# Attention on one Trainium2 core: one K chunk transposed by DMA, the loads in another order, and a new opening list

## The chip, the core and the metric

The kernel runs on one core of a Trainium2 chip. The metric is device microseconds of one execution. A core has five engines that run their own instruction streams and wait for each other by semaphores: TensorE (PE, matmuls and the loading of their weights), VectorE (DVE), ScalarE (ACT), GpSimd (POOL) and SyncE (SP), and DMA queues that SP, ACT and POOL fill. Matmuls write to PSUM, which has eight banks of 128 x 512 float32; ACT and DVE read and free them.

## What is computed

```python
"q", "k", "v": np.random.randn(8, 2048, 512).astype(np.float32)

d_k = q.shape[-1]
scores = np.matmul(q, k.transpose(0, 2, 1)) / np.sqrt(d_k)
attn_weights = special.softmax(scores, axis=-1).astype(np.float32)
return np.matmul(attn_weights, v)
```

Eight batches of attention, 2048 queries and keys of width 512, no mask.

## The kernel before

Everything is float16 on the way into PE and float32 in PSUM. Each batch's queries are cut into two spans of 1024, each span into two halves of 512. The scores are made transposed, with 128 keys on the partitions and 512 queries along a row, so that their exponentials can go straight into the second matmul as weights. K of a batch is four chunks (`kraw`, c = 0 to 3) of four blocks of 128 keys; Q is four such chunks, of which two make a span (`qraw`, one tile for each span). Both come as rows and have to be transposed, d onto the partitions.

**Seven products for eight.** A group (class `Group`, line 311) takes two key blocks and both halves of a span's queries. As a 2 x 2 block product over two halves of d it would be eight products of two matmuls; the kernel uses the form with seven, whose operands are sums. Sums of K are `k_sums(c)` (line 191: `ks`, and one in place in `kraw`), those of Q `q_sums(sp)` (line 208: `qs`, and one in place or in a spare room). Product 1 goes to a bank x; a copy puts it into a second bank y as well (`after1`); 6, 7 and 4 are added on x and 2 on y; 5 and 3 make z. After 5, z is copied to a float32 tile `cz` in SBUF (`after5`, line 362), after 6 x is copied beside it (`after6`, line 365), two adds on DVE (`after7`, `after3`, lines 368 and 371) finish the right half, and exponentials on ACT (line 279) write `left` (queries of the first half, from x and y) and `right` (second half, one wide exponential from `cz`, `exp_right`). A span has eight groups. In the first span of the first batch the sums aren't there yet when PE starts, so its first eight key blocks (chunks 0 and 1) are made without them, by `plain_eighth` and by `plain_tile` (line 281, four matmuls of 512 columns); groups 0 to 3 of the opening's steps are the other four pairs of blocks of span 0 (chunk 2 in groups 0 and 1, chunk 3 in groups 2 and 3), groups 4 to 11 are span 1.

**The second matmul** (P times V) works on two columns a and b of 128 queries of either half, also in seven products: words a1 to a7 and b1 to b7 (line 455), with sums of V (`v_sums`, line 223) and of P (`p_sums`, line 384). From the second pair of columns on, three of the seven are split once more (`fine`, line 649, words s, t, u).

**Banks.** `bank(name)` (line 83) hands out a bank from a pool: "qx" (2), "qy" (1), "qz" (1), "px" (2) and "pz" (2, also as "py"). A group's x came from "qx"; `own` said whether y and z came from the q or the p pools: p for groups 1 and 3, q for all others. `COPIES` held two letters for each group of span 0: which engine, ACT or DVE, copies y and z; x was always copied by ACT, and in span 1 all three were.

**Start.** Rows of chunk 0 come in single blocks. Then POOL's queue (lines 871 to 876) loads K chunk 1, Q chunk 1, Q chunk 2, K chunk 2, Q chunk 3, K chunk 3, the last five as 512 KB each into rooms that `left` and `right` of span 1 will use later (`spare`), so that in the profile these chunks have the names `right` and `left`. Q and K chunks 0 and 1 and K chunks 2 and 3 are transposed by PE (`transposed`, line 165: four 128 x 128 transposes for each block, and a copy from PSUM by DVE or ACT, line 173). Q chunks 2 and 3, needed by span 1, are transposed by SP's DMA queue, two halves each (`dma_transpose`, line 156, issued at line 160). POOL then copies one element of Q chunk 2's first half (`gate`, line 914); the four loads of V (line 221) stand behind that copy in POOL's queue.

**The opening list.** Up to the second pair of columns the order is written out by hand in `OPENING` (line 746), word by word (`word`, line 944), and each engine runs its own part of it in order. `*` is one step of `score()`: the next of the seven products in the order of `QORDER`, where products 7 and 4 of a group come between those of the next; the first steps of that kind with no group before are empty. `TK2.0.2ax` transposes K chunk 2 from block 0, two blocks, copied by a (ACT) or d (DVE), bank from x, z, p or q ("qx", "pz", "px", "qz"). `t6.1p` is the plain tile of key block 6, second half. `k21` and `q02` are sums (chunk 2, number 1; span 0, number 2), v, X, Y, Z sums of V, A, B, N sums of P; `a1<` and `a1>` are the two halves of product a1 over the keys; a 1 in front means the second pair of columns. From the third pair of columns (about 84 us) tables set the order; they repeat for the rest of the run and are the same in both kernels.

Of the kernel before, what the change touches and what calls it, by code (L numbers as in the profile page):

```python
# [12 lines left out]
def kernel(  # L13
# [21 lines left out]
    nc = tc.nc  # L35
# [16 lines left out]
    NJ = NKB // 2  # L52
# [5 lines left out]
    NG = NJ // 2  # L58
# [24 lines left out]
    def bank(name):  # L83
        name = "pz" if name == "py" else name
        t = psum[name].tile([P, 512], F32, tag=name)
        return t
# [37 lines left out]
    def load(what, b, c, pieces=(CH,), room=None):  # L124
        t = staged.get((what, b, c))
        if room is not None:
            t = staged[what, b, c] = room
        if t is None:
            t = staged[what, b, c] = stage.tile([P, CH, D], F16, tag="stage", name="stage")
        n = CH - sum(pieces)  # L130
        for w in pieces:
            at = c * CH + n
            nc.gpsimd.dma_start(out=t[:, n:n + w, :], in_=srcs[what][b, :, at:at + w, :])  # L133
            n += w
# [21 lines left out]
    def dma_transpose(what, b, c, h):  # L156
        src = staged.pop((what, b, c)) if h else staged[what, b, c]
        dst = raw_of(what, b, c)
        ns = slice(h * CH // 2, (h + 1) * CH // 2)
        nc.sync.dma_start_transpose(  # L160
            out=dst[:, ns].rearrange("p n c r -> p (n c) r"),
            in_=src[:, ns].rearrange("p n d -> p (n d)"),
        )
# [147 lines left out]
    class Group:  # L311


        def __init__(self, sp, j):
            self.sp, self.j = sp, j
            self.own = "q" if sp or j % 2 == 0 or j < NG else "p"

        def product(self, n):
            c, j = divmod(self.j, 2)
            a11, a12, a21, a22 = k_blocks(c)  # L320
            b11, b12, b21, b22 = q_blocks(self.sp)
            _, s1, s2, s4 = kops[c]
            t1, t2, t4 = qsum
            t3 = t3_of(self.sp)
            if n == 1:
                if self.sp not in pts:
                    new_p(self.sp)
                self.left, self.right = pts[self.sp][0:2]
                self.x = bank("qx")
            elif n == 5:  # L330
                self.z = bank(self.own + "z")
            lhs, rhs, dst = {
                1: (a11, b11, "x"),
                2: (a12, b21, "y"),
                3: (s4, b22, "z"),
                4: (a22, t4, "x"),
                5: (s1, t1, "z"),
                6: (s2, t2, "x"),
                7: (a21, t3, "x"),
            }[n]  # L340
            dst = getattr(self, dst)
            for dc in range(2):
                nc.tensor.matmul(  # L343
                    dst[:], lhs[:, j, dc, :], rhs[:, :, dc, :],
                    start=(n in (1, 5) and dc == 0), stop=(dc == 1),
                    skip_group_check=True,
                )
            getattr(self, f"after{n}", lambda: None)()
# [5 lines left out]

        def copy(self, n):

            by = "a" if self.sp else COPIES[2 * (self.j - 2) + n]
            return nc.scalar.copy if by == "a" else nc.vector.tensor_copy

        def after5(self):  # L360
            self.cz = czpool.tile([P, 2, QH], F32, tag="cz", name="cz")
            self.copy(1)(out=self.cz[:, 1, :], in_=self.z[:])  # L362

        def after6(self):
            nc.scalar.copy(out=self.cz[:, 0, :], in_=self.x[:])  # L365

        def after7(self):
            nc.vector.tensor_add(self.cz[:, 1, :], self.x[:], self.cz[:, 1, :])  # L368
# [160 lines left out]
    class Fine(Pair):  # L529
# [4 lines left out]
        early = False  # L534
# [192 lines left out]
    def placed(text):  # L727
# [14 lines left out]
        "a7'@1 b7'@2 a4'@5 u1@5 b4'@9 u2@10 s1@12 u3@12 s2@13 u4@14 s3@15 a3@15 s4@17 b3@18 "  # L742
        "a6@19 t1@23 b6@24 t2@24 t3@25 t4@27",
    )
    COPIES = "aadaaaadadad"
    OPENING = (
# [9 lines left out]
    )  # L756

    ENDS = {
# [100 lines left out]
    for n in range(1, CH):  # L859
# [5 lines left out]
    spare = [  # L865
        t[:].rearrange(form + " -> p (" + form[2:] + ")")[:, i * CH * D:(i + 1) * CH * D]
        .rearrange("p (n d) -> p n d", n=CH)
        for t, form, n in ((pts[1][1], "p j s q", 4), (pts[1][0][0], "p j q", 2))
        for i in range(n)
    ]  # L870
    load("k", 0, 1, (2, 2))
    load("q", 0, 1, room=spare[0])
    load("q", 0, 2, room=spare[2])
    load("k", 0, 2, room=spare[1])
    load("q", 0, 3, room=spare[5])
    load("k", 0, 3, room=spare[3])
    gate = const.tile([P, 1], F32)
    firsts["v"] = lambda: [load_v(0, c) for c in range(NCH)]
    nc.gpsimd.memset(vt1[:, :, H:H + 1], 1.0)
# [28 lines left out]
    plain_eighth(1, 1, 0)  # L908
    transposed("k", 1, 1, 1, dve)
    plain_eighth(1, 1, 1)  # L910
    for c in (2, 3):
        for h in range(2):
            dma_transpose("q", 0, c, h)
    nc.gpsimd.tensor_copy(out=gate[:], in_=qraw[1][:, 1, ND - 1, 0:1])  # L914
    firsts.pop("v")()

# [2 lines left out]

    prev = cur = None  # L920
    steps = [0]
    early = {}

    def score():

# [18 lines left out]
    def word(w):  # L944

        copies = {"d": dve, "a": act}
        rooms = {"x": "qx", "q": "qz", "p": "px", "z": "pz"}
        n = [int(x) for x in w if x.isdigit()]
        for _ in range(len(later)):
            later.popleft()()  # L950
        if w == "*":
            score()
        elif w[0] == "1":
            (pv if w[1] in "abstu" else sum_of)(1, w[1:])
        elif w[0] in "gR":
            if n[0] not in early:
                early[n[0]] = Group(0, n[0])
            if w[0] == "R":
                early[n[0]].exp_right()
            else:  # L960
                early[n[0]].product(n[1])
        elif w[0] == "t":
            plain_tile(n[0], n[1], rooms[w[-1]])
        elif w[0] == "T":
            transposed(w[1].lower(), n[0], n[1], n[2], copies[w[-2]], rooms[w[-1]])
        elif w[0] == "k":
            k_sums(n[0])[n[1]]()
        elif w[0] == "q":
            q_sums(n[0])[n[1]]()
        elif w[0] == "v":  # L970
            v_sums(0, n[0])[n[1]]()
        elif w[0] in "AB":
            part = {"<": (0, NG), ">": (NG, NJ)}.get(w[-1], (0, NJ))
            p_sums(0, w[0].lower(), *part)[n[0]]()
        elif w[0] in "XYZ":
            vi_sums(0, "XYZ".index(w[0]))[n[0]]()
        elif w[0] == "N":
            p_sums(1, "ab")[n[0]]()
        else:
            pv(0, w)  # L980
# [66 lines left out]
```

## Time and profile before

| | |
|---|---|
| median of 3 runs | 785.38 us (784.53 to 785.4) |
| the profiled execution, whole | 784.17 us |
| its span, first to last instruction | 782.4 us |
| DVE busy, 0 to 50 us of the span | 34.39 us |
| DVE busy, 50 to 100 us | 47.89 us |
| ACT busy, 50 to 100 us | 41.26 us |
| POOL's copies wait for Q chunk 2 | 16.7 us |
| moved by DMA | 117.65 MB, 150 GB/s mean |

The span is what the profile's rows are counted in; the execution is 1.8 us longer. Rows of a timeline give start and length in microseconds, then engine, line, operation, what it writes and reads, and how many were merged; a bracket at the end gives the idle time just before and who ended it. PE's own times are modelled from its starts, and matmuls overlap, so the distance from start to start is the safer measure.

### The profile page before, as it was taken

To read this page: it belongs to the slowest core of one execution; us is meant where nothing else is said; L and a number is where in the kernel's file an instruction comes from. 1 tells how busy PE (TensorE), PEld (TensorE's weight loads), DVE (VectorE), ACT (ScalarE), POOL (GpSimd) and SP (SyncE) were. 2 spreads that over 40 slices of the span, in tenths; PEclk is the share of its full clock that TensorE was granted. 3 is DMA by queue.
4 is the path that set the end of the run, shared out by engine and by line. 5 is a ranking of instruction groups with operands and counts; after the bars stand their busy time and mean duration, and the time that the engine had idled before them with its cause. 6 is when DMAs were issued, how large, how long until landed. Compare 5 with 4: busy or idle time off the path is not lost.

```text
span 782.4 us, 18227 instructions
## 1 busy us (share of the span) xinstructions
PE 776.1 (99%) x6598; PEld 534.6 (68%) x6598; DVE 718.9 (92%) x1605; ACT 643.6 (82%) x1339; POOL 116.1 (15%) x157
## 2 busy tenths in 40 slices
PE   8999999999999999999999999999999999999998
PEld 5467666676666666666766666676676666666677
DVE  3899999989999899998999989999899998999886
ACT  4888888888888888888888888888888888888873
POOL 4111112012021120211102121021210212100000
PEclk9999999999999999999999999999999999999999
DMA  9999993999939997499956999379993999932113
GB/s 187 188 156 164 160 202 73 191 181 189 177 56 199 177 193 147 84 186 191 193 118 113 180 185 193 100 140 191 163 191 92 152 176 187 202 62 61 49 49 115
DMA packets 212410, 117.65 MB, mean 150 GB/s; under 512 B 128480, under 2 KB 212064, under 8 KB 212320
## 3 DMA queue, kind: packets, MB, share of 16 engines
q0 software_dynamic: 52528, 51.91, 46.0%
q1 hardware_dynamic: 159504, 64.26, 42.0%
q8 instruction: 51, 0.84, 0.5%
q14 instruction: 39, 0.32, 0.1%
q10 hardware_dynamic: 288, 0.33, 0.1%
HBM read 100.73 MB, written 33.55 MB: 172 GB/s over the span
## 4 chain that ended last, share of the span: by engine, by line
PE 94%; DMA 4%; POOL 1%; issue 0%; ACT 0%; POOLq 0%
PE t L343 46%; PE t L455 30%; PE t L676 18%; DMA vh<-in_v_dram 2%; DMA right<-in_q_dram 1%; DMA qraw<-right 1%; POOL first L861 0%; POOL vh L221 0%; POOL stage L133 0%; POOL right L133 0%; ACT o L464 0%; POOL gate L914 0%; POOLq L1031 0%
## 5 line engine op out<-in xcount | busy, mean ns | idle before, releaser
L343 PE MATMUL t<-qraw,kraw 128*128 128x512 f16 x736 | 200.1, 379 | 0.2 <-ACT left L279 0.2
L464 ACT ACTIVATE o<-t,r 128x256 f32<-128x256 f32 x300 | 136.8, 480 | 71.3 <-DVE r L490 25.5
L279 ACT ACTIVATE left<-t 128x512 f16<-128x512 f32 (+1 forms) x260 | 154.2, 600 | 15.7 <-PE t L343 7.7
L343 PE MATMUL t<-qs,ks 128*128 128x512 f16 x496 | 140.7, 379 | 0.0
L279 ACT ACTIVATE right<-cz 128x1024 f16<-128x1024 f32 x124 | 131.9, 1064 | 3.5 <-DVE cz L368 3.4
L343 PEld LDWEIGHTS <-kraw 128*128 128x128 f16 x992 | 88.9, 97 | 58.9 <-issue 0.8
L455 PEld LDWEIGHTS <-right 128*128 128x128 f16 x1024 | 99.7, 98 | 33.4
L455 PEld LDWEIGHTS <-s 128*128 128x128 f16 x1056 | 100.4, 97 | 29.0
L676 PEld LDWEIGHTS <-si 128*128 128x128 f16 x1044 | 76.3, 97 | 36.4 <-issue 0.2
L343 PEld LDWEIGHTS <-ks 128*128 128x128 f16 x744 | 69.1, 97 | 42.2 <-issue 0.9
L362 ACT COPY cz<-t 128x512 f32<-128x512 f32 x121 | 70.9, 586 | 31.8 <-PE t L343 30.3
L371 DVE TENSOR_TENSOR cz<-t,cz 128x512 f32<-128x512 f32 x124 | 85.0, 686 | 9.5 <-ACT o L464 4.1
L368 DVE TENSOR_TENSOR cz<-t,cz 128x512 f32<-128x512 f32 x124 | 84.8, 684 | 5.8 <-PE t L343 5.2
L676 PEld LDWEIGHTS <-left 128*128 128x128 f16 x976 | 69.5, 97 | 21.2
L467 DVE SCALAR_TENSOR_TENSOR o<-t,r,o 128x256 f32<-128x256 f32 x148 | 69.3, 479 | 12.5 <-ACT ci L696 7.5
L353 ACT COPY t<-t 128x512 f32<-128x512 f32 x124 | 72.5, 584 | 3.8 <-PE t L343 0.6
L343 PE MATMUL t<-qraw,ks 128*128 128x512 f16 x248 | 73.6, 378 | 0.2 <-DVE cz L362 0.2
L343 PE MATMUL t<-qs,kraw 128*128 128x512 f16 x248 | 73.7, 379 | 0.0
L365 ACT COPY cz<-t 128x512 f32<-128x512 f32 x124 | 72.2, 583 | 0.3
L676 PE MATMUL t<-vh,left 128*128 128x128 f16 x732 | 70.8, 219 | 0.0
L455 PE MATMUL t<-vt,s 128*128 128x256 f16 (+1 forms) x544 | 70.5, 273 | 0.0
L455 PE MATMUL t<-vh,s 128*128 128x257 f16 x512 | 66.7, 273 | 0.0
(116 smaller groups left out, 1202.8 us busy)
## 6 DMA issues: line engine op xcount, KB each, us to landing
out_dram<-o SPq DMA_DIRECT2D x256, 128.0 KB, 3.8
vh<-in_v_dram POOLq DMA_DIRECT2D x32, 512.0 KB, 9.5
stage<-in_q_dram POOLq DMA_DIRECT2D x28, 512.0 KB, 7.2
stage<-in_k_dram POOLq DMA_DIRECT2D x28, 512.0 KB, 8.3
o<-o POOLq DMA_DIRECT2D x14, 128.0 KB, 2.7
right<-in_q_dram POOLq DMA_DIRECT2D x2, 512.0 KB, 9.8
right<-in_k_dram POOLq DMA_DIRECT2D x2, 512.0 KB, 14.8
qraw<-stage SPq DMA_TRANSPOSE x56, 6.4
```

The costliest lines, as they stand in the source:

```text
L279: nc.scalar.activation(out=out_, in_=in_, func=EXP, scale=inv_sqrt_d)
L343: nc.tensor.matmul(dst[:], lhs[:, j, dc, :], rhs[:, :, dc, :], start=(n in (1, 5) and dc == 0), stop=(dc == 1), skip_group_check=True,)
L353: self.copy(0)(out=self.y[:], in_=self.x[:])
L362: self.copy(1)(out=self.cz[:, 1, :], in_=self.z[:])
L365: nc.scalar.copy(out=self.cz[:, 0, :], in_=self.x[:])
L368: nc.vector.tensor_add(self.cz[:, 1, :], self.x[:], self.cz[:, 1, :])
L371: nc.vector.tensor_add(self.cz[:, 0, :], self.z[:], self.cz[:, 0, :])
L455: nc.tensor.matmul(dst[:, 0:width], lhs(j), rhs(j), start=(first and j == 0), stop=(j == NJ - 1), skip_group_check=True,)
L464: nc.scalar.activation(out=out_, in_=src, func=COPY, scale=r[:])
L467: nc.vector.scalar_tensor_tensor(out=out_, in0=src, scalar=r[:], in1=out_, op0=MULT, op1=ADD)
L676: nc.tensor.matmul(dst, lhs[:, j, :], rhs[:, j, :], start=(n == 1 and j == 0), stop=(j == NI - 1), skip_group_check=True,)
```

## The change

1. POOL loads K chunks 2 and 3 ahead of Q chunks 2 and 3.
2. K chunk 3 is transposed by SP's DMA queue, ahead of the two Q chunks. Its two words with 16 PE transposes and two DVE copies leave the list.
3. `OWNS` and `XOWNS` give each of the twelve groups of the first batch its pools for y and z and for x; `COPIES` has three letters for each, so x may be copied by DVE too. Groups 0 and 2 take x from "px"; groups 1 and 4 take y and z from "pz". DVE copies z of group 2 and x of group 10, all others are ACT's.
4. `OPENING` is laid anew. Behind Q chunk 1, two plain tiles (t6.0, t7.0) stand ahead of K chunk 2's first half, where five did (t7.0, t6.1, t1.1, t4.1, t0.1); the sums of K chunk 0, of V and of P, the plain tiles and the products of the second matmul stand in other places.
5. Code for two kinds of words that no list uses (g and R) is dropped.

```diff
--- before.py
+++ after.py
@@ -313,7 +313,10 @@
 
         def __init__(self, sp, j):
             self.sp, self.j = sp, j
-            self.own = "q" if sp or j % 2 == 0 or j < NG else "p"
+            n = sp * NJ + j - NG
+            self.by = COPIES[3 * n:3 * n + 3] if sp < 2 else "aaa"
+            self.own = OWNS[n] if sp < 2 else "q"
+            self.xown = XOWNS[n] if sp < 2 else "q"
 
         def product(self, n):
             c, j = divmod(self.j, 2)
@@ -326,7 +329,7 @@
                 if self.sp not in pts:
                     new_p(self.sp)
                 self.left, self.right = pts[self.sp][0:2]
-                self.x = bank("qx")
+                self.x = bank(self.xown + "x")
             elif n == 5:
                 self.z = bank(self.own + "z")
             lhs, rhs, dst = {
@@ -354,15 +357,14 @@
 
         def copy(self, n):
 
-            by = "a" if self.sp else COPIES[2 * (self.j - 2) + n]
-            return nc.scalar.copy if by == "a" else nc.vector.tensor_copy
+            return nc.scalar.copy if self.by[n] == "a" else nc.vector.tensor_copy
 
         def after5(self):
             self.cz = czpool.tile([P, 2, QH], F32, tag="cz", name="cz")
             self.copy(1)(out=self.cz[:, 1, :], in_=self.z[:])
 
         def after6(self):
-            nc.scalar.copy(out=self.cz[:, 0, :], in_=self.x[:])
+            self.copy(2)(out=self.cz[:, 0, :], in_=self.x[:])
 
         def after7(self):
             nc.vector.tensor_add(self.cz[:, 1, :], self.x[:], self.cz[:, 1, :])
@@ -742,17 +744,19 @@
         "a7'@1 b7'@2 a4'@5 u1@5 b4'@9 u2@10 s1@12 u3@12 s2@13 u4@14 s3@15 a3@15 s4@17 b3@18 "
         "a6@19 t1@23 b6@24 t2@24 t3@25 t4@27",
     )
-    COPIES = "aadaaaadadad"
+    COPIES = "aaaaaaadaaaaaaaaaaaaaaaaaaaaaaaadaaa"
+    OWNS = "qpqqpqqqqqqq"
+    XOWNS = "pqpqqqqqqqqq"
     OPENING = (
-        "TK1.2.1dz t5.0x TK1.3.1az t4.0x TQ1.0.2dp TQ1.2.1az TQ1.3.1dz t7.0x k10 q00 q01 t6.1p "
-        "t1.1z t4.1z t0.1p TK2.0.2ax TK2.2.2dp t3.1x k12 k20 * k22 k23 q03 t5.1z * * * t6.0x k21 "
-        "* t2.1p k00 k02 q02 * * TK3.0.2dz * * TK3.2.2dp * k30 * k32 k01 * * * * k33 * * k03 k13 "
-        "* k31 * t7.1p * * * * * v00 * a1< * q10 * * q11 * A0< * * v01 q12 b1< * * q13 * a1> * * "
-        "v02 v10 * * b1> * A0> X0 A1 k11 v11 * a5 A3 * * * X1 * a3 B0 A2 B1 v12 * * a2 B3 * * B2 "
-        "* a6 * b5 * v03 v13 X3 * 1Z1 1Z3 * * X2 b3 * * b2 N0 * 1z1 1a7' * b6 * 1Z2 1S2 1z2 1u1 * "
-        "1z3 1b7' * * * 1a4' * 1z4 1x1 1Z4 * * * 1S3 1b4' * 1u2 1S4 1x2 1k01 1s1 * 1u3 * 1x3 * "
-        "1s2 1y1 1u4 1x4 1k02 * 1a3 1y2 * 1Y1 1s3 1b3 1k03 1k04 1Y2 1y3 * 1t1 * 1N1 * 1s4 * 1Y3 "
-        "1a6 1Y4 1t2 1y4 * * * 1b6 * * 1N3 1t3 * * 1q1 1t4 1q2"
+        "TK1.2.1dz t5.0z TK1.3.1az t4.0p TQ1.2.1dp TQ1.0.2dx TQ1.3.1dz t6.0x t7.0p k10 TK2.0.2az "
+        "k12 t1.1z k00 q00 TK2.2.2dx t0.1p k20 q01 * * k22 t6.1z k21 * q02 k23 * * t5.1z q03 * * "
+        "* * * t3.1q * * * * * k30 * k32 k02 t4.1x * t2.1z k33 * * k31 * * k01 * * * * q10 q12 "
+        "t7.1p q11 * * * * A0< k13 * k03 v00 * * * b1< a1< v02 q13 * * A0> * * * v01 A1 v10 * * * "
+        "* a1> a5 A3 B0 * * k11 B1 * a3 v12 v11 * * X0 * B3 a2 a6 * * * b5 N0 * 1Z1 * b1> 1z1 * "
+        "A2 B2 b3 v13 * * * X1 * X3 b6 v03 * 1Z3 1S2 * * 1b7' b2 * 1S3 * 1Z2 * 1u1 1b4' 1z2 1a7' "
+        "* 1u2 * 1x1 1Z4 1z4 * * 1z3 1S4 1x3 1a4' 1u3 * * X2 * 1x2 1s1 1u4 * 1k01 1a3 1s2 1Y1 1x4 "
+        "* 1k02 * 1Y2 * 1y1 * * 1s3 1y2 1b3 1t1 1Y3 1y3 1s4 1y4 * 1k03 * 1k04 1t2 * 1q1 1N1 1t3 "
+        "1a6 * 1Y4 1b6 1q2 * 1t4 * 1N3 *"
     )
 
     ENDS = {
@@ -870,10 +874,10 @@
     ]
     load("k", 0, 1, (2, 2))
     load("q", 0, 1, room=spare[0])
+    load("k", 0, 2, room=spare[1])
+    load("k", 0, 3, room=spare[3])
     load("q", 0, 2, room=spare[2])
-    load("k", 0, 2, room=spare[1])
     load("q", 0, 3, room=spare[5])
-    load("k", 0, 3, room=spare[3])
     gate = const.tile([P, 1], F32)
     firsts["v"] = lambda: [load_v(0, c) for c in range(NCH)]
     nc.gpsimd.memset(vt1[:, :, H:H + 1], 1.0)
@@ -908,9 +912,9 @@
     plain_eighth(1, 1, 0)
     transposed("k", 1, 1, 1, dve)
     plain_eighth(1, 1, 1)
-    for c in (2, 3):
+    for what, c in (("k", 3), ("q", 2), ("q", 3)):
         for h in range(2):
-            dma_transpose("q", 0, c, h)
+            dma_transpose(what, 0, c, h)
     nc.gpsimd.tensor_copy(out=gate[:], in_=qraw[1][:, 1, ND - 1, 0:1])
     firsts.pop("v")()
...
```

Three places of the program, as its rows stand. First POOL's queue, from the loads of whole chunks to the copies that hold back V; `right` and `left` are the rooms, `qraw_116` is Q of span 1, `vh_120` V. Before:

```order
L133 DMA right<-in_q_dram 128x4x512 x2
L133 DMA right<-in_k_dram 128x4x512
L133 DMA left<-in_q_dram 128x4x512
L133 DMA right<-in_k_dram 128x4x512
L879 MEMSET vt_122 128x8
L880 MEMSET ui_128 128x4
L881 MEMSET vh_120 128x8
L914 CAST gate<-qraw_116 128x1
L221 DMA vh_120<-in_v_dram 128x4x512 x4
```

Now:

```order
L133 DMA right<-in_q_dram 128x4x512
L133 DMA right<-in_k_dram 128x4x512 x2
L133 DMA right<-in_q_dram 128x4x512
L133 DMA left<-in_q_dram 128x4x512
L883 MEMSET vt_122 128x8
L884 MEMSET ui_128 128x4
L885 MEMSET vh_120 128x8
L918 CAST gate<-qraw_116 128x1
L221 DMA vh_120<-in_v_dram 128x4x512 x4
```

K chunks 2 and 3 are second and third of these five loads, where they were third and fifth; V still waits for Q chunk 2.

Second, SP's queue from its start; `kraw_111` is K chunk 3, the next batch's chunks come from `stage`. Before:

```order
L140 DMA cz<-in_q_dram 128x512
L160 DMA_TRANSPOSE qraw_116<-right 128x8x128 x2
L160 DMA_TRANSPOSE qraw_116<-left 128x8x128 x2
L160 DMA_TRANSPOSE qraw_115<-stage 128x8x128 x2
L160 DMA_TRANSPOSE kraw_99<-stage 128x8x128
```

Now:

```order
L140 DMA cz<-in_q_dram 128x512
L160 DMA_TRANSPOSE kraw_111<-right 128x8x128 x2
L160 DMA_TRANSPOSE qraw_116<-right 128x8x128 x2
L160 DMA_TRANSPOSE qraw_116<-left 128x8x128 x2
L160 DMA_TRANSPOSE qraw_115<-stage 128x8x128 x2
L160 DMA_TRANSPOSE kraw_99<-stage 128x8x128
```

Two halves of K chunk 3 stand ahead of the four halves of Q.

Third, DVE around the first sums of chunk 3 (`ks_3_112`). Before, from the third sum of Q of span 0 (line 214) on:

```order
L214 TENSOR_TENSOR left<-qraw_115 128x1024
L371 TENSOR_TENSOR cz<-t,cz 128x512
L173 COPY kraw_111<-tr 128x1024
L368 TENSOR_TENSOR cz<-t,cz 128x512
L173 COPY kraw_111<-tr 128x1024
L362 COPY cz<-t 128x512
L195 TENSOR_TENSOR ks_3_112<-kraw_111 128x512
L197 TENSOR_TENSOR ks_3_113<-ks_3_112,kraw_111 128x512
```

Now:

```order
L214 TENSOR_TENSOR left<-qraw_115 128x1024
L198 TENSOR_TENSOR ks_2_110<-kraw_107,ks_2_109 128x512
L215 TENSOR_TENSOR qs_119<-qraw_115,qs_118 128x1024
L373 TENSOR_TENSOR cz<-t,cz 128x512
L370 TENSOR_TENSOR cz<-t,cz 128x512
L373 TENSOR_TENSOR cz<-t,cz 128x512
L195 TENSOR_TENSOR ks_3_112<-kraw_111 128x512
L370 TENSOR_TENSOR cz<-t,cz 128x512
L197 TENSOR_TENSOR ks_3_113<-ks_3_112,kraw_111 128x512
```

The two copies of chunk 3 and the copy of z after them (of group 1) are gone from here; the first sum of chunk 3 has the add of group 1's z (line 373) in front of it.

More of the change, by code (lines that the diff above doesn't have):

```diff
@@ L921 @@
     steps = [0]
-    early = {}
     def score():
@@ L954, in word @@
             (pv if w[1] in "abstu" else sum_of)(1, w[1:])
[L955 to L961, printed above, removed]
         elif w[0] == "t":
```

## The prediction, made before the changed kernel ran

> **What bounds the kernel now.** I read the page first: the busy times and the shares of the chain.
>
> ```profile
> PE 776.1 (99%) x6598; PEld 534.6 (68%) x6598; DVE 718.9 (92%) x1605; ACT 643.6 (82%) x1339; POOL 116.1 (15%) x157
> PE 94%; DMA 4%; POOL 1%; issue 0%; ACT 0%; POOLq 0%
> ```
>
> TensorE is busy for 776.1 of 782.4 us, and the chain that ended last is TensorE for 94%. So the time changes only by matrix work that goes away, or by waits of PE. Next, the table by stretch, since the change lies in the opening (to about 84 us).
>
> ```profile
> core 0: us, PE busy (x) PEld busy (x) DVE busy (x) ACT busy (x) POOL busy (x), PEclk, DMA share, GB/s
> 10.00:20.00 10.00, 9.77 (x75) 5.46 (x73) 3.92 (x8) 6.57 (x15) 0.01 (x1) 1.00 1.24 206
> 20.00:30.00 10.00, 9.74 (x69) 5.29 (x70) 7.84 (x16) 7.79 (x13) 3.16 (x5) 1.00 1.25 185
> 30.00:40.00 10.00, 9.82 (x47) 4.48 (x47) 8.99 (x19) 8.49 (x15) 0.24 (x1) 1.00 1.18 192
> 40.00:50.00 10.00, 9.83 (x61) 5.75 (x60) 9.91 (x21) 8.19 (x15) 2.51 (x6) 1.00 0.70 115
> 50.00:60.00 10.00, 10.00 (x72) 6.70 (x70) 9.64 (x21) 8.42 (x15) 0.75 (x1) 1.00 1.23 196
> ```
>
> PE has small holes from 10 to 50 us and none in the next ten; the clock is 1.00 throughout; VectorE (DVE) is nearly full from 40 us on. The holes, in PE's timeline (start, length, instruction; in brackets the idle time the profile sees):
>
> ```profile
> 13.36 1.03 PE L286 MATMUL t<-qraw,kraw 128*128 128x512 f16 x4
> 14.53 1.07 PE L170 MATMUL tr<-ident,right 128*128 128x128 f16 x16
> 15.43 4.48 PE L286 MATMUL t<-qraw,kraw 128*128 128x512 f16 x20
> 20.03 1.07 PE L170 MATMUL tr<-ident,right 128*128 128x128 f16 x16
> 23.95 1.89 PE L286 MATMUL t<-qraw,kraw 128*128 128x512 f16 x8
> 25.68 0.59 PE L343 MATMUL t<-qraw,ks 128*128 128x512 f16 x2
> 26.54 0.61 PE L170 MATMUL tr<-ident,right 128*128 128x128 f16 x8
> 26.99 0.59 PE L343 MATMUL t<-qraw,kraw 128*128 128x512 f16 x2
> 29.16 0.59 PE L343 MATMUL t<-qs,kraw 128*128 128x512 f16 x2
> 29.99 0.59 PE L343 MATMUL t<-qraw,ks 128*128 128x512 f16 x2 [0.24 <-DVE cz L362]
> 37.92 0.59 PE L343 MATMUL t<-qraw,kraw 128*128 128x512 f16 x2
> 38.69 0.59 PE L343 MATMUL t<-qraw,kraw 128*128 128x512 f16 x2 [0.18 <-ACT left L279]
> 41.71 0.38 PE L455 MATMUL t<-vh,left 128*128 128x256 f16 x2
> 42.26 0.38 PE L455 MATMUL t<-vh,left 128*128 128x256 f16 x2 [0.17 <-DMA vh<-in_v_dram]
> 45.51 1.06 PE L455 MATMUL t<-vt,s 128*128 128x257 f16 x8
> ```
>
> Matmuls overlap, so I count from start to start: eight 512-column matmuls from 23.95 to 25.68, 0.216 us each. A product of two is 0.43 us, a plain tile of four 0.86, eight transposes 0.45 (26.54 to 26.99). By that count PE loses 0.31 us before 14.53 (Q chunk 1), 20.03-15.43-20x0.216 = 0.27 before 20.03 (K chunk 2), 29.99-29.16-0.43 = 0.40 (a copy on DVE), 38.69-37.92-0.43 = 0.34 (an exponential that frees a bank), and 0.33 before 42.26 (the last V load; two 256-column matmuls are 0.22).
>
> **What is removed.** Chunk 3 of K needs 16 transposes less on PE: 2 x 0.45 = 0.90 us, straight off the bound. The two copies they fed leave DVE. Of the five waits, the first stays (Q chunk 1 still lands first). The other four lose their cause: K chunk 2 is awaited elsewhere (below); the DVE copy at 29.99 stood behind the two copies of chunk 3; the group that waited at 38.69 now takes a bank that was free earlier; V is awaited elsewhere. That is 0.27+0.40+0.34+0.33 = 1.34 us to be had.
>
> **What is added on PE.** I count the new list from 14.53. Sixteen transposes of Q and two plain tiles end at 14.53+0.90+1.73 = 17.16; then the list wants K chunk 2, now second in the load queue. The chain of waits gives when the second load landed, and what hung on it.
>
> ```profile
> 6.74 11.10 DMA right<-in_q_dram
> 17.86 8.79 DMA qraw<-right
> 26.94 2.21 POOL vh L221 x3
> 29.14 13.08 DMA vh<-in_v_dram
> ```
>
> The second load (Q chunk 2 then) landed at 6.74+11.10 = 17.84, the third (K chunk 2) by 20.0 by the PE row. All are 512 KB, so K chunk 2 now lands at 17.84 and PE waits 17.16 to 17.88: **+0.72**. Bound below: first to third took 14.5 to 20.0, 2.75 each, which would give 17.25 and a wait of 0.1. I take the row of the slot itself.
>
> Two halves of chunk 2 and two plain tiles (2.62) bring PE to 20.50; twelve products and three plain tiles (7.77) bring it to 28.27, where group 2 first reads chunk 3; 30.0 is where it needs the first sum of chunk 3, and 38.2 where group 4's product 6 needs the copy of its x. That copy stands on ScalarE (ACT) behind group 2's wide exponential, a copy and three exponentials: the sequence that before has from 32.65 on, first and last row here.
>
> ```profile
> 32.65 1.06 ACT L279 ACTIVATE right<-cz 128x1024 f16<-128x1024 f32 x1 [0.51 <-DVE cz L368]
> 35.52 0.62 ACT L353 COPY t<-t 128x512 f32<-128x512 f32 x1
> L371 DVE TENSOR_TENSOR cz<-t,cz 128x512 f32<-128x512 f32 x124 | 85.0, 686 | 9.5 <-ACT o L464 4.1
> L173 DVE COPY kraw<-tr x5: 425/681/692, 11.8 to 28.7; 128x1024 f16<-128x1024 f16 x3, 128x512 f16<-128x512 f16 x2
> ```
>
> It took 35.52+0.62-32.65 = 3.49 us. The wide exponential needs the add behind product 7 of group 2, which PE issues from 33.5 to 33.9; with the add's 0.69 and some 0.2 at the handover (estimated from the overlap of the matmuls) it can begin near 34.9 and the sequence ends at 38.4: **+0.3**, between 0 and 0.6 for a handover that is nothing or double.
>
> **The transfers.** Chunk 3's two halves go through SP's transposing queue ahead of the four halves of Q. Its load is third now and lands at 20.0, so SP starts 2.1 us later than it did at 17.86. The landings below are those of `right` (to 30 us), `left` (to 35) and `vh` (to 44), from issue.
>
> ```profile
> 17.86 5.43 SPq L160 DMA_TRANSPOSE qraw<-right  x2
> 23.32 4.38 SPq L160 DMA_TRANSPOSE qraw<-left  x2
> L160 SPq DMA_TRANSPOSE qraw<-right x2: 1353/2684/4015, 17.9 to 19.3; - x2
> DMA to landing us min/median/max: 8.3/9.9/17.1
> DMA to landing us min/median/max: 5.1/5.3/14.5
> DMA to landing us min/median/max: 7.1/10.1/13.1
> GB/s 0 39 347 277 142 195 161 186 185 201 204 208 203 206 213 201 204 209 206 203 196 199 163 138 286 239 86 67 200 191 201 191 211 195 204 206 204 45 0 0
> ```
>
> Halves landed at 17.86+8.79 = 26.65, 19.3+8.3 = 27.6, 23.32+5.1 = 28.4 and (issued about 26.4) 31.7. The last load was under way until 8.9+17.1 = 26.0, and the rate (slices of 1.1 us from 0 to 44 us) jumps to 286 GB/s at 26.4. So the first half did not need 8.8 us, it waited for the loads; then a half takes about 0.9. The new first two therefore land at about 26.7 and 27.6, before 28.27 and before DVE takes up the sums at about 29: **0**. Were the 8.8 and 8.3 their own length, they would land at 28.8 and 29.7: +0.5 at 28.27, and about +0.4 more at 30.0.
>
> The queue behind them matters more. The load of V stands on POOL behind a copy that reads the first half of Q chunk 2, which is the third half now: 28.4 at best (the old third), 30.5 if all shifts by 2.1, against 26.65. From that copy to V's last landing it took 42.22-26.65 = 15.57 us, so V is complete at 44.0 to 46.1; up to 0.9 more if a further half falls into its way, since three halves follow now, and one did. Without that wait PE would reach the second half of a1 (word a1>) at 38.5+5.6 = 44.15. It waits from nothing to 2.8; with the copy at 29.0, and a little for sharing, V is there at 44.9: **+0.7**. On DVE the second half's V sums (v10) wait in the same place, and the group adds stand behind them. V's first half is the second of four loads; with the first at 26.9+7.1 = 34.0 and the last at 42.2, 2.7 apart, it landed at 36.7, so some 39.1 now; it is needed at 39.4. Q's last half, 31.7 before and some 33 to 35 now, is needed at 34.7 by the Q sums on DVE. I count both at zero, with up to 0.8 against.
>
> **From 45 us to the end of the list** the sums, copies and products stand in another order. DVE has some 1.6 us less in all, by durations: the two K copies go (0.69 each, the DVE row above), of three copies of z or x one goes (taken at the add's 0.69), and one copy of a single Q block comes (0.42). I found no place where a sum comes after its product by the count, but DVE covers this with little room (9.64 of 10); at the tightest, the sum for u2, the margin is some 0.3. Zero, up to 0.5 against. From the third pair of columns on the program is the old one.
>
> **Sum.** -0.90-1.34+0.72+0.3+0.7 = -0.5 us. The profiled execution took 784.17, so its like would take 783.7; it lies 1.2 below the median of 785.38, and the forecast is against the median: **784.9**. A difference of 0.2% (1.6 us) is about what can be told from none here.
>
> **Rivals.**
>
> *The loads keep time* (22%). K chunk 2 lands at its mean pace (wait 0.1), V's gate opens at 28.4 (wait 0.1): -0.5-0.62-0.6 = -1.7, 783.7; with the 0.3 gone too, 783.4. For it: the pace of 2.75 us and the 286 GB/s. Against it: the slot's own 17.84, and six halves where there were four.
>
> *Slower: V late behind the transposes* (25%). The gate opens at 30.5, and one more half shares V's first microseconds: V complete at 47.0, PE waits 2.8 instead of 0.7, and K3's 0.5 comes with the same shift: -0.5+2.1+0.5 = +2.1, 787.5. It decides for slower once V is complete after about 46.3. For it: the start 2.1 us later, and SP's second issue that took 4.0 us with loads under way. Against it: the loads end at 26.0 in either order.
>
> *Nothing gained* (51% together with the forecast, within 0.2%). The new waits eat the 0.90 whole, for instance K3's halves at 28.8 and 29.7: -0.5+0.9 = +0.4, 785.8.
>
> *A transposing transfer is no match for PE* (2%, in the slower). If the halves could not overlap, each 8.8 us after the one before, chunk 3 would be whole at 20.0+17.6 = 37.6, and its sum, needed at 30.0, would hold PE about 8 us: 793. The landings at 26.65, 27.6 and 28.4 speak against it. Beside it stands the Trainium skill, VectorE: DVE Perf Modes, section The three transpose paths: 390 ns for a 128x128 block on TensorE against 1309 ns by DMA, and TensorE as the choice where PSUM will do. By that page, as an estimate, 16 blocks by DMA one after the other would be 20.9 us and the change a loss; the halves 0.9 us apart, 8 blocks each, do not agree with it.
>
> **How the numbers follow.** Faster 0.22, same 0.51, slower 0.27. The range goes from 783.3 (loads on time, all of it) to 787.2 (most of V late); the likeliest case alone spans 783.9 to 785.9.
>
> **What would show it.** 32 transposes from `right` in the profile after, not 48, and none of the DVE copies that followed them. A PE wait of 0.7 us for `right<-in_k_dram` near 17.2, or 0.1. The first half of kraw landing before 28.3, the copy that gates V near 29, a wait for vh near 44. Wrong if PE waits for kraw, if the gate opens after 30, or if after 50 us PE waits for a sum of DVE; and wrong in the other direction if neither chunk 2 nor V holds PE.

## The result, and the profile after

The changed kernel takes **792.0 us** (median of 6 runs, 791.2 to 792.9) against 785.2 us of the kernel before, measured beside it (784.5 to 785.8). The ratio is 1.0084, with a 95% interval of 1.0068 to 1.0100: slower by some 6.8 us, where 784.9 us and at most 787.2 was forecast. The profiled execution took 792.14 us, its span is 790.4 us, 8.0 more than the 782.4 of the profile before.

Where does it go? First the table by stretch, in the same columns as before.

```profile
core 0: us, PE busy (x) PEld busy (x) DVE busy (x) ACT busy (x) POOL busy (x), PEclk, DMA share, GB/s
0.00:34.00 34.00, 31.76 (x209) 18.56 (x210) 18.10 (x39) 20.85 (x39) 12.11 (x25) 1.00 1.09 183
34.00:52.00 18.00, 12.97 (x46) 5.13 (x44) 8.68 (x16) 8.55 (x15) 3.40 (x7) 0.72 1.05 149
52.00:780.00 728.00, 728.00 (x6263) 506.49 (x6262) 687.08 (x1539) 611.21 (x1281) 100.55 (x125) 1.00 0.86 149
```

From 52 us on PE is busy without a hole. All of the loss lies before, and most of it from 34 to 52 us, where PE issues 46 matmuls in 18 us and the mean granted clock is 0.72. PE's timeline there, and the finer stretches of the clock:

```profile
15.06 1.89 PE L286 MATMUL t<-qraw,kraw 128*128 128x512 f16 x8
17.85 0.62 PE L170 MATMUL tr<-ident,right 128*128 128x128 f16 x8 [0.89 <-DMA right<-in_k_dram]
...
37.47 0.59 PE L346 MATMUL t<-left,kraw 128*128 128x512 f16 x2
41.94 1.01 PE L346 MATMUL t<-qs,ks 128*128 128x512 f16 x2 [3.88 <-DVE qs L212]
43.27 1.03 PE L346 MATMUL t<-qs,ks 128*128 128x512 f16 x2 [0.32 <-DVE qs L213]
45.14 1.01 PE L346 MATMUL t<-qs,kraw 128*128 128x512 f16 x2 [0.83 <-DVE cz L370]
45.95 1.91 PE L457 MATMUL t<-vh,left 128*128 128x256 f16 x8
47.65 1.06 PE L346 MATMUL t<-qraw,ks 128*128 128x512 f16 x2
48.51 2.58 PE L346 MATMUL t<-qraw,kraw 128*128 128x512 f16 x6
50.92 1.03 PE L346 MATMUL t<-qs,ks 128*128 128x512 f16 x4
51.87 0.38 PE L346 MATMUL t<-qs,kraw 128*128 128x512 f16 x1
```

```profile
38.00:40.00 2.00, 0.06 (x1) 0.00 (x0) 0.00 (x0) 0.47 (x1) 0.00 (x0) 1.00 1.72 151
40.00:42.00 2.00, 0.06 (x1) 0.06 (x1) 0.77 (x2) 0.00 (x0) 0.69 (x1) 0.63 1.01 167
48.00:50.00 2.00, 2.00 (x6) 0.73 (x5) 1.02 (x2) 0.40 (x1) 0.62 (x2) 0.50 0.80 125
50.00:51.00 1.00, 1.00 (x4) 0.37 (x3) 0.00 (x0) 0.69 (x2) 0.00 (x0) 0.61 1.23 206
51.00:52.00 1.00, 1.00 (x6) 0.41 (x5) 0.88 (x2) 0.47 (x2) 0.00 (x0) 1.00 1.25 205
```

Counted from start to start as in the prediction: from 37.47 to 51.87 are 20 matmuls of 512 columns and 8 of 256, 20 x 0.216 + 8 x 0.109 = 5.19 us of work in 14.40 us. **9.21 us are lost.** PE waits 4.04 us for the Q sum of L212, and then, with a product of two at 0.85 us (half the pace), 0.48 and 1.02 us: 5.54 us of waits. The other 3.67 us are the clock. It was granted at 1.00 until about 40.5 us, some 2.5 us after PE had run dry, at 0.50 until about 50.8 (0.61 as the mean of 50 to 51 leaves the full clock only the last 0.2 us), and at 1.00 from there. With the 1.06 us that PE waits for K chunk 2 (15.06 + 8 x 0.216 to 17.85), less the 0.90 and 1.34 that the change removes, the sum is 8.03 us, the 8.0 of the spans. So close a fit is partly luck: smaller items are left out, such as Q chunk 1's transposes, which PE reached 0.37 us earlier (14.16 against 14.53), and they happen to cancel.

Why was the sum late? The chain of waits of the kernel after goes back from L212, which reads from both halves of Q chunk 3, to the transfers (`issue` rows left out). The row of L212 itself stands below it:

```profile
7.45 12.57 DMA right<-in_k_dram
...
20.03 1.34 SPq L160
...
21.43 3.68 SPq L160
...
25.16 1.31 SPq L160
...
26.51 1.35 SPq L160
...
27.91 1.32 SPq L160
...
29.27 11.84 DMA qraw<-left
...
41.20 0.70 DVE qs L212
```

```profile
41.20 0.69 DVE L212 TENSOR_TENSOR qs<-qraw 128x1024 f16<-128x1024 f16 x1 [6.45 <-DMA qraw<-left]
```

K chunk 3's load landed at 20.02, SP issued six halves one after the other, and the last of them, issued at 29.27, took 11.84 us to land. DVE had stood before this sum since 34.75 (41.20 less 6.45). In the profile before, the last half was issued at 26.4 and landed 5.3 us later:

```profile
L160 SPq DMA_TRANSPOSE qraw<-left x2: 1312/2171/3030, 23.3 to 26.4; - x2
DMA to landing us min/median/max: 5.1/5.2/5.3
```

What differs is its place against V. POOL's rows, after:

```profile
28.54 0.18 POOL L918 CAST gate<-qraw 128x1 f32<-128x1 f16 x1 [18.54 <-DMA qraw<-right]
28.77 2.98 POOL L221 DMA_DIRECT2D vh<-in_v_dram  x4
```

The gate opens on the first half of Q chunk 2, which was the first of four halves and is now the third of six. Then V's four loads leave at 28.77, and the last half is issued 0.50 us **behind** the first of them. Before, it was issued 0.54 us **ahead** (26.4 against 26.94). What that means for the packets, from 32 to 38 us after, and in the one microsecond from 27 to 28 before:

```profile
q0 software_dynamic: 898, 0.90, 89.4%
q1 hardware_dynamic: 840, 0.22, 27.2%
```

```profile
q1 hardware_dynamic: 1120, 0.28, 125.1%
```

q1 carries the transposes, in packets of 256 bytes, q0 V in packets of 1 KB. Alone, q1 moved 1120 packets in a microsecond, about one half (256 KB, so 1,024 of them). Beside V it moved 840 in six, one for each packet of V (898). This agrees with the Trainium skill, DMA: Bandwidth & Descriptors, section Queues, rings and completion order, by which a DMA engine takes its queues in turn, packet by packet. Here the queue of small packets got half of the turns and a fifth of the bytes (0.22 of 1.12 MB).

### The profile page after: what moved, and what is told of

It is laid out like the page before. It is cut to its first block, busy times and chain, and to the rows that moved or that the text cites. A ratio compares the mean times of both kernels' runs of the same rounds, so it can differ in the third digit from the quotient of the medians.

```text
span 790.4 us, 18191 instructions
## 1 busy us (share of the span) xinstructions
PE 779.4 (99%) x6582; PEld 536.0 (68%) x6582; DVE 717.5 (91%) x1603; ACT 643.3 (81%) x1339; POOL 116.1 (15%) x157
## 4 chain that ended last, share of the span: by engine, by line
PE 94%; DMA 3%; SPq 1%; POOL 1%; DVE 0%; issue 0%; ACT 0%; DVEq 0%; POOLq 0%
PE t L346 46%; PE t L457 30%; PE t L678 18%; DMA right<-in_k_dram 2%; DMA qraw<-left 1%; SPq L160 1%; POOL first L865 0%; POOL stage L133 0%; POOL right L133 0%; DVE qs L212 0%; DVE cz L373 0%; DVE cz L370 0%; ACT o L466 0%; DVE ks L198 0%; DVE s L401 0%
## 5 line engine op out<-in xcount | busy, mean ns | idle before, releaser
L469 DVE SCALAR_TENSOR_TENSOR o<-t,r,o 128x256 f32<-128x256 f32 x148 | 69.1, 478 | 12.2 <-ACT ci L698 7.5
```

The source lines that it names most:

```text
L469: nc.vector.scalar_tensor_tensor(out=out_, in0=src, scalar=r[:], in1=out_, op0=MULT, op1=ADD)
```

## The experiments

Theory A, formed from the traces: V's packets overtake the last Q half, DVE and then PE wait for it, and the idle PE loses its clock; the rest of the change is worth about nothing. The rivals put the loss in the new list, in K chunk 3's transfers themselves, or in a late V. All kernels are the kernel after with the edit shown, unless said otherwise, and each was timed beside the kernel before (785.1, 785.0 and 784.9 us in the three sessions). Of the rows of the list an edit shows only the words around it.

**Keep the clock.** Eighteen matmuls on a constant, whose result nobody reads, stand where PE ran dry.

```diff
-  k13 * k03 v00 * * * b1< a1<
+  k13 * k03 v00 I99 * * * b1< a1<
+        elif w[0] == "I":
+            dummies["px"] = bank("px")
+            idle(sum(n), "px")
```

> The change, with 18 matmuls of 512 columns on the zero tile put in front of group 4's product 5, where PE stood still from 38.1 to 41.9 us; they add nothing to the result. Theory A (late half of Q chunk 3, then a lower clock): the half still lands near 41 and group 4's product 5 still starts near 41.9, but PE has worked through the wait, the clock stays at 1.00, and the 3.5 us that matmuls at half clock cost from 41.9 to 50.6 go: about 788.5. Theory B (the list, its banks and its copies are slow in themselves, and the clock is a side effect): no change, 792, or slower by the 3.9 us of matmuls put in. Theory C (the granted clock falls for another reason than the idle PE): clock 0.5 at 42 to 50 us as before, 792.

790.5 us (788.4 to 791.0), ratio 1.0065 [1.0047, 1.0083]; span 788.2. The mean clock is 1.00, and the same products read:

```profile
38.27 4.05 PE L890 MATMUL t<-warm 128*128 128x512 f16 x18
42.64 0.59 PE L346 MATMUL t<-qs,ks 128*128 128x512 f16 x2 [0.32 <-DVE qs L212]
43.97 0.60 PE L346 MATMUL t<-qs,ks 128*128 128x512 f16 x2 [0.74 <-DVE qs L213]
45.84 0.59 PE L346 MATMUL t<-qs,kraw 128*128 128x512 f16 x2 [1.26 <-DVE cz L370]
46.27 1.03 PE L457 MATMUL t<-vh,left 128*128 128x256 f16 x8
```

The clock is a loss of its own, but only some 2 of its 3.67 us come back (2.2 between the spans, 1.5 between the medians). PE at full pace waits longer for the same sums of DVE (0.48, 0.90 and 1.44 us, start to start), and the half landed later here, at 29.2 + 12.6 = 41.8. The other three runs had a mean clock of 0.998 to 0.999, so in them a little of it may still be lost. The late half remains.

**V behind all of Q.** Both gate copies ahead of V's loads, so that these wait for the last half's landing.

```diff
     nc.gpsimd.tensor_copy(out=gate[:], in_=qraw[1][:, 1, ND - 1, 0:1])
+    nc.gpsimd.tensor_copy(out=gate[:], in_=qraw[1][:, 2 * NT - 1, ND - 1, 0:1])
     firsts.pop("v")()
-    nc.gpsimd.tensor_copy(out=gate[:], in_=qraw[1][:, 2 * NT - 1, ND - 1, 0:1])
```

> The change, but V's loads wait for the last half of Q chunk 3, not for the first of Q chunk 2. Theory A: the last half lands near 32.5 (1.33 us after the one before), the Q sums on DVE start at 35, and the wait of 4.0 us at group 4's product 5 is gone with the lower clock; V is then issued about 3.8 us later, its second load lands near 42.4 and its last near 47.7, and PE waits 2 to 3.5 us for it in two places: 787 to 788.5. Theory B: 791 or more, as the list is the same. If V's lateness cost as much as Q's did, 792.

787.4 us (785.9 to 788.6), ratio 1.0025 [1.0012, 1.0039]. In the profiled run (786.9 us) the last half lands 3.1 us after its issue, PE waits for no Q sum and the clock stays at 1.00. Of the median 4.6 us come back. Now V is late, issued at 34.03, and PE waits 2.2 us for it, start to start. The clock was 1.00 in four of the ten runs, which took 785.9 to 786.9 us; in the six others, of 787.3 to 788.6, its mean was 0.997 or 0.998, that is some 3 to 5 us at half pace. So part of what is left in the median is clock again.

**The new list without the transfers of K chunk 3.** PE transposes chunk 3 again, SP only Q.

```diff
-    for what, c in (("k", 3), ("q", 2), ("q", 3)):
+    for what, c in (("q", 2), ("q", 3)):
-  * * * t3.1q * * * * * k30
+  * * * t3.1q TK3.0.2dx * * * TK3.2.2dx * * k30
```

> The change without its transposing transfer: K chunk 3 by 16 PE transposes and two DVE copies again (behind t3.1 and two products later), SP's queue with the four halves of Q alone; loads, banks, copy letters and the rest of the new list as in the change. Theory A: the four halves land near 26.4, 27.3, 28.6 and by 32, Q sums start at 35, V is complete by about 43, so neither Q nor V holds PE; 0.9 us of transposes come back and the wait for K chunk 2 of 1.0 stays: 785.0, the same as before, clock 1.00. Theory B: still 789 or more.

787.5 us (786.2 to 788.4), ratio 1.0025 [1.0007, 1.0042]: above what I gave. The profile tells why. Q's loads are the last two now, so SP starts on them only at 22.84; the last half was issued at 26.99, V at 26.86, and the half was overtaken again (a row of the chain of waits, then one of POOL's):

```profile
26.99 11.23 DMA qraw<-left
```

```profile
26.86 2.98 POOL L221 DMA_DIRECT2D vh<-in_v_dram  x4
```

PE waited 0.6, 0.9 and 1.4 us (start to start) for the sums and the add behind them, and lost some clock. So the kernel was no test of the list alone; the load order by itself brings on the conflict.

**The same, with the one plain half that does not need K chunk 2 (t1.1z) ahead of its transposes.**

```diff
-  t7.0p k10 TK2.0.2az k12 t1.1z k00
+  t7.0p k10 t1.1z TK2.0.2az k12 k00
```

> As the run with K chunk 3 by PE, and the plain tile t1.1 (0.86 us) moved in front of K chunk 2's first transposes, where PE waited 1.0 us for the load. If that wait is the price of the new load order, 0.7 to 0.9 us less than that run, 784.2; if PE only meets it later (ACT and DVE late with the copies), the same as that run.

788.2 us, but spread from 785.1 to 796.1; ratio 1.0042 [1.0017, 1.0067]: with this spread not to be told from the run without the edit. In the profiled run, one of the quickest (785.6), the half was overtaken as well (issued 27.27, landed 37.6) and yet DVE waited only 0.28 us for it and PE not at all: the first load of Q had held PE 1.6 us at the start, and the clock was at half from about 8.8 to 12.2 us. What an overtaken half costs depends on how far PE has come. The run of 796.1 was not profiled, and its cause is open.

**V behind the issue of the last half only.** The gate reads the first half of Q chunk 3, the fifth of six.

```diff
-    nc.gpsimd.tensor_copy(out=gate[:], in_=qraw[1][:, 1, ND - 1, 0:1])
+    nc.gpsimd.tensor_copy(out=gate[:], in_=qraw[1][:, NT + 1, ND - 1, 0:1])
```

> The kernel after with one index changed: the tiny copy on POOL that lets V's loads go waits for the first half of Q chunk 3 (landed at 31.2 us in the kernel after) and not for the first half of Q chunk 2 (28.5 us). The last half is issued at about 29.3 us, so it now goes ahead of V's first load, which is issued at about 31.6 us. Theory A (the whole loss comes from V's packets overtaking the last Q half, and the rest of the change is worth about nothing): the last half lands near 32.5 us, no wait of DVE for it, the granted clock stays at 1.00, V's four chunks land 2.3 us earlier than in the run with both gate copies ahead (there 39.72, 42.95, 45.50, 48.05 us) and PE's wait for V, 2.2 us there, goes to under 0.5: 784.5 to 785.8 us. Rival (V, let go 2.7 us later, is late by about as much as it was in that run): PE waits 1.5 to 2.2 us for V, 786.5 to 787.5 us.

785.8 us (785.2 to 787.1), ratio 1.0008 [0.9999, 1.0017]: one index brings back 6.2 of the 6.8 us. The last half lands 3.1 us after its issue at 29.52 and the Q sum of L212 starts at 34.25, without a wait:

```profile
34.25 0.68 DVE L212 TENSOR_TENSOR qs<-qraw 128x1024 f16<-128x1024 f16 x1
```

The time is theory A's, at its upper edge, but the wait for V did not go as theory A had it; it was the rival's:

```profile
38.96 0.38 PE L457 MATMUL t<-vh,left 128*128 128x256 f16 x2
41.20 0.81 PE L457 MATMUL t<-vh,left 128*128 128x256 f16 x6 [1.85 <-DMA vh<-in_v_dram]
```

V's second chunk was issued at 32.48 and took 8.67 us, to 41.15. I had moved the landings with the issue (2.3 us ahead of the run with V behind all of Q, 42.95 there) and got 1.8.

**The list with K chunk 3 on PE and that gate**, and **the same with t1.1z ahead** (the last pair of lines in the second alone).

```diff
-    for what, c in (("k", 3), ("q", 2), ("q", 3)):
+    for what, c in (("q", 2), ("q", 3)):
-    nc.gpsimd.tensor_copy(out=gate[:], in_=qraw[1][:, 1, ND - 1, 0:1])
+    nc.gpsimd.tensor_copy(out=gate[:], in_=qraw[1][:, NT + 1, ND - 1, 0:1])
-  * * * t3.1q * * * * * k30
+  * * * t3.1q TK3.0.2dx * * * TK3.2.2dx * * k30
-  t7.0p k10 TK2.0.2az k12 t1.1z k00
+  t7.0p k10 t1.1z TK2.0.2az k12 k00
```

> The new list with K chunk 3 transposed by PE, as in the earlier run of 787.48 us, and V's loads let go by the first half of Q chunk 3, which landed at 28.9 us there, behind the issue of the last half at 27.0 us. Theory A says the residue of that run was the same overtaking (last half issued 0.13 us behind V's first load, landed 38.2 us, 3.0 us of waits of PE and 1.7 us at a lower clock): the last half lands near 30 us, the waits for the Q sums and the clock loss go, 783.5 to 785.3 us. Rival (that residue came from the new order of the copies and banks, not from the last half): waits for the Q sums and for a copy stay, 786.5 to 788 us.

> The same, with the one score half that does not need K chunk 2 (t1.1z) put ahead of its first transposes. Theory A: as the run before it, less what PE waits for K chunk 2 (0.1 to 1.4 us by how PE stands against the loads), so 783.3 to 785.0 us, and the wide scatter of the run without the later gate (783.3 to 794.4 us of span) goes with the overtaking. Rival (the scatter comes from the first loads, which vary from run to run): the median is the same within 1 us but runs still scatter by more than 4 us.

783.9 us (783.3 to 788.6), ratio 0.9992 [0.9978, 1.0006], and **783.3 us** (782.8 to 783.8), ratio 0.9977 [0.9967, 0.9986], both as theory A gave: the second beats both kernels. PE's timeline of it, in the place where the kernel after stood still:

```profile
37.45 0.59 PE L346 MATMUL t<-left,kraw 128*128 128x512 f16 x2
37.88 1.22 PE L346 MATMUL t<-qs,ks 128*128 128x512 f16 x4
38.94 0.59 PE L346 MATMUL t<-qs,kraw 128*128 128x512 f16 x2
39.37 1.04 PE L457 MATMUL t<-vh,left 128*128 128x256 f16 x8
40.25 0.59 PE L346 MATMUL t<-qraw,ks 128*128 128x512 f16 x2
```

There is no wait but 0.20 us (38.94 - 37.88 - 4 x 0.216). Only the gate differs from the two kernels of 787.5 and 788.2 us, and the scatter of the second went with it (1.0 us in place of 11), against the rival that put it down to the first loads alone; of the first, one run in ten still took 788.6. And with the same gate, K chunk 3 by transfers is 1.9 us **slower** than on PE (785.8 against 783.9): two halves more ahead of Q let V go at 31.74 and not at 29.40, which costs PE 2.0 us of waiting and saves 0.90 of transposes. That accounts for 1.1 of the 1.9; where the rest goes was not taken apart.

**The transfers alone, with the old list.** The kernel before, its load order and SP's six halves as after, chunk 3's transposes out of the list.

```diff
+    load("k", 0, 2, room=spare[1])
+    load("k", 0, 3, room=spare[3])
     load("q", 0, 2, room=spare[2])
-    load("k", 0, 2, room=spare[1])
     load("q", 0, 3, room=spare[5])
-    load("k", 0, 3, room=spare[3])
-    for c in (2, 3):
+    for what, c in (("k", 3), ("q", 2), ("q", 3)):
-  k00 k02 q02 * * TK3.0.2dz * * TK3.2.2dp * k30
+  k00 k02 q02 * * * * * k30
```

> The kernel before with its own opening list, banks and copiers, and only the transfers of the change: K loaded ahead of the second span's Q, K chunk 3 transposed by two transfers that go ahead of Q's four, and its 16 transposes on PE left out of the list. Theory A (the loss lies in the transfers, whatever the list): V's first load again leaves ahead of the last Q half, which lands at 38 to 42 us in place of 31.7; the list asks for it at 37.7 us (the sums on DVE) so that PE waits some 2 to 5 us and the clock may fall: 787 to 792 us. Rival (the new list is what made the late half cost so much, the old one has cover for it): 784 to 786 us.

790.2 us (789.4 to 791.1), ratio 1.0063 [1.0048, 1.0078]. The transfers cost most of the loss under the old list too. But PE waits for the other party:

```profile
36.91 0.38 PE L455 MATMUL t<-vh,left 128*128 128x256 f16 x2 [0.84 <-DMA vh<-in_v_dram]
40.38 0.45 PE L455 MATMUL t<-vh,left 128*128 128x256 f16 x2 [3.10 <-DMA vh<-in_v_dram]
```

The half again left behind V and landed at 42.2; sharing the engines, V's second chunk landed at 40.34, and the old list asks for it at 37.1 (36.91 and two matmuls of 0.109). The clock was at half from about 40.6 to 44.0 here. The two streams slow each other, and the list decides which of them holds PE.

**The kernel before with V 0.6 us earlier.** Its gate reads the end of K chunk 3's load.

```diff
-    nc.gpsimd.tensor_copy(out=gate[:], in_=qraw[1][:, 1, ND - 1, 0:1])
+    nc.gpsimd.tensor_copy(out=gate[:], in_=staged["k", 0, 3][:, CH - 1, D - 1:D])
```

> The kernel before with one argument changed: the tiny copy on POOL that lets V's loads go reads the last element of K chunk 3's load (landed at 26.01 us) and not the first half of Q chunk 2 (26.65 us). V's first load is then issued at about 26.3 us, just ahead of the last Q half (26.40 us), and not 0.54 us behind it. Theory A (the order of these two issues decides, in either kernel): the last half lands at 36 to 39 us in place of 31.7, V's second chunk at 37.5 to 38.5 in place of 36.5, the list asks for both near 37.7 us, and the time is 785.5 to 788.5 us. Rival (0.6 us earlier is only 0.6 us earlier, the half's data goes first all the same): the half lands near 32 us, V 0.6 us earlier than before, and the time is 784.5 to 785.2 us.

```profile
L160 SPq DMA_TRANSPOSE qraw<-left x2: 1327/2213/3099, 23.7 to 26.8; - x2
DMA to landing us min/median/max: 5.1/7.9/10.7
```

```profile
26.75 2.98 POOL L221 DMA_DIRECT2D vh<-in_v_dram  x4
```

The order turned by 0.05 us, and the last half took 10.7 us in place of 5.3 and landed at 37.5 in place of 31.7, as theory A has it. The time, 785.1 us, ratio 1.0009 [0.9997, 1.0022], is the rival's: the old list starts this sum at 37.69 us, so that nothing waited for the half, and PE's wait for V rose only from 0.2 to 0.6 us. The overtaking is the same in both kernels; the price is set by the need.

**The gate of 785.8 us, with t1.1z ahead.**

```diff
-    nc.gpsimd.tensor_copy(out=gate[:], in_=qraw[1][:, 1, ND - 1, 0:1])
+    nc.gpsimd.tensor_copy(out=gate[:], in_=qraw[1][:, NT + 1, ND - 1, 0:1])
-  t7.0p k10 TK2.0.2az k12 t1.1z k00
+  t7.0p k10 t1.1z TK2.0.2az k12 k00
```

> The kernel with V let go by the first half of Q chunk 3 (785.84 us, K chunk 3 by transfers), and the one score half that does not need K chunk 2 (t1.1z) put ahead of its first transposes, which took away PE's wait of 0.6 to 0.9 us at 17 us where V was not late. Theory A (in this kernel V's second chunk, at 41.15 us, sets the end of the opening: PE waits 1.9 us for it): what is won ahead of it is lost in a longer wait, 785.4 to 786.2 us. Rival (V's landing moves with the rest, or the wait is not on the path): 784.6 to 785.2 us.

785.7 us (784.8 to 786.9), ratio 1.0010 [1.0001, 1.0019]. The median is theory A's: no gain shows here, where with V in time the same edit went with a gain of 0.6 us (783.9 to 783.3). But theory A's reason is not shown. PE's wait for V's second chunk did not grow: it is 2.0 us in both profiles, and V landed 0.20 us earlier (40.95). In the profile without the edit PE had been held by the first loads and did not wait for K chunk 2, so there was nothing to win in it. The clock plays a part: it was 0.998 or lower in five of the eleven runs, and in two of the ten without the edit. The runs at 1.00 took 784.8 to 785.7 us with the edit and 785.2 to 786.2 without, which looks like the rival's small gain. What takes it from the median is open.

## Why the prediction was wrong

**What held.** 16 transposes less on PE (32 rows from `right`). K chunk 2 landed at 17.8 (17.84 said), PE waited 1.06 us (0.72 said), as Q chunk 1 came earlier and PE with it. K chunk 3's halves landed at 26.4 and 27.3 and nothing waited for them, so the transposing transfers did not go one after the other at 8.8 us each. The gate opened at 28.54 (29.0 taken), V was whole at 45.6 (44.9 taken, 44.0 to 46.1). The copy that group 4's product 6 needs costs 0.20 us where nothing else is late (0.3 said). From 52 us on no sum is late. So none of the signs that I had named for being wrong came; the miss lay where I had set none.

**What failed** is the sentence "Q's last half, 31.7 before and some 33 to 35 now, is needed at 34.7 ... I count both at zero, with up to 0.8 against". It was needed at 34.75, as said; it came at 41.12. I had moved its landing by the shift of SP's queue and added a little for sharing. I had charged the sharing to V ("a further half falls into its way") and never asked what V does to the half. The profile before held a hint: its last half took 5.3 us with no load left under way, where a half alone lands in 3.1 to 3.4, and its last 41 packets passed between 29 and 32 us, as V's began. The two issue times stood in the rows that I quoted, 26.4 and 26.94: the change turns their order, since one of them hangs on the third half of six and the other on SP's pace. The kernel with the gate two halves later (785.8 us against 792.0) shows that this is the cause; the kernel before with V moved ahead of the half by 0.05 us shows the landing turn with it.

**What was missing** is the clock. None of my cases had PE wait 4 us for a Q sum, and none, not even the one that holds PE for 8 us, carried the 3.67 us of half-speed matmuls behind it, of which keeping PE busy brought back some 2.

**The rivals.** "Slower: V late behind the transposes" had the place, but the wrong victim at first: it was Q's half that was late. With the order mended V's second chunk, not its last, holds PE 2.0 us; I had counted that chunk at zero (39.1, needed at 39.4), and it came at 41.15, from a gate that lets V go 3.0 us later than the change does (31.74 against 28.77). By that kernel the change without the overtaking is 785.8 us, my "nothing gained" to the tenth, but with a V wait of 2.0 in place of 0.7.

## What to carry to other kernels

Where two queues feed one deadline, write down the issue time of each transfer and see whether the change turns their order; here a transfer that left 0.50 us behind the other stream cost 6 us, and in the kernel before, which needs it later, the same turn cost nothing clear of noise. A gate that holds one stream back should open on an event that lies behind the issue of the last transfer it must not disturb, not on one that happened to come at the right moment, and no later than that, since the held stream has its own deadline (787.4 against 785.8 us). A hole of a few microseconds in PE also has to be charged with the slow matmuls that follow it.

## What the runs showed of the hardware

A transposing transfer of some 1,000 packets of 256 bytes landed 3.1 to 3.4 us after its issue where no other stream was under way. The last half of Q took 10.3 to 12.9 us in each of the six profiles in which it left 0.04 to 0.50 us behind V's first load of 1 KB packets, and 5.3 us in the kernel before, where it left 0.54 us ahead. While both moved, both got about the same number of packets (840 and 898 in 6 us).

The granted clock fell about 2.5 us after PE ran dry (38.06 to about 40.5) and came back near 50.8, after PE had been busy from 45.14 on, 5.6 us. The Trainium skill, TensorE: Matmul & The Clock Gate, Part 1, gives a free-running window of about 3.4 us for both. The return lies within two such windows; the fall came after less than one window of idleness. The stretches at half clock have the window's length: 10.24 us here (40.53 to 50.77, worked out from the mean clock of slices of 0.1 and 0.2 us), three times 3.41; 3.41 us in the run with K chunk 3 on PE and the early gate (42.84 to 46.25), 3.41 with the transfers alone and the old list, and 3.4 at the start of the run of 788.2 us. Each such stretch costs, as an estimate, up to 1.7 us of matmul work.

In the run with K chunk 3 on PE and the early gate it fell with no hole over 1.3 us in the profile, after three that it puts at 0.48, 0.74 and 1.26 us within 4.3 us:

```profile
42.00:43.00 1.00, 0.71 (x4) 0.41 (x4) 1.00 (x3) 0.73 (x1) 0.00 (x0) 0.92 0.43 73
43.00:44.00 1.00, 1.00 (x7) 0.74 (x5) 0.96 (x3) 1.00 (x3) 0.77 (x2) 0.50 0.00 0
```

So a window need not be empty here. Holes of 0.32, 0.74 and 1.26 us behind the constant matmuls did not lower it in the profiled run; what tells the two apart was not tried.
